# Hybrid attention / Mamba-2 kernel: tile 0's time steps inside layer 0's last output projection, and a first front that begins with context and tile 0

## The chip, the cores and the metric

The kernel runs on one core of one Trainium2 chip. The metric is device microseconds of one execution. A profile of one execution, taken by the hardware profiler, gives every instruction with its engine: PE (TensorE matmuls), DVE (VectorE), ACT (ScalarE), POOL (GpSimd) and SP (SyncE, whose queue issues most of the DMAs). Each engine takes its instructions in the order in which the program holds them.

## The reference

Two layers over a latent stream of 1024 tokens and a context of 256, model width 1024, all in float32. Layer 0 is gated windowed attention, layer 1 a bidirectional Mamba-2 (SSD) mixer. Each layer normalizes, modulates, mixes, and adds with a gate. What the change touches is the end of layer 0 and the beginning of layer 1:

```python
y, yc = attention_mixer(u, uc, ...)          # ends with (o * silu(g)) @ w_out
h = h + gate[:, None] * y
...
u = rms_normalize(h) * (1.0 + scale[:, None]) + shift[:, None]      # layer 1
...
z, xbc, dt_raw = jnp.split(h @ w_in, [SSD_WIDTH, SSD_WIDTH + SSD_CONV_DIM], axis=-1)
xbc = jax.nn.silu(centred_depthwise_conv(xbc, conv_w, conv_b))
xs, bm, cm = jnp.split(xbc, ...)
dt = jax.nn.softplus(dt_raw + dt_bias_dir)   # time steps: 2 directions x 32 heads
...
da = dt_d * a_dir[d]
a_cs = jnp.cumsum(da, axis=2)                # within chunks of 128 tokens
states = einsum(bm, exp(a_last - a_cs), xdt)
y_diag = (C B^T * exp(a_cs_q - a_cs_s)) @ xdt;  y_off = C @ h_prev * exp(a_cs)
```

The time steps `dt` of all tokens (64 rows: two directions by 32 heads) are needed by every one of the eight SSD groups; a group has four heads, 256 columns of x and of the gate z, and 128 each of B and C.

## The kernel before

**Tiling.** Tokens form three tiles, `TT`: latent tile 0 (512 tokens), latent tile 1 (512) and the context (256). The normalized, modulated stream of a layer is held as two parts in a reduced-precision format, `uH` and `uL`, one pair for each tile, with the model width on the partitions in eight slices; every projection multiplies high by high, high by low and low by high, so a product over width 1024 takes 24 matmuls for each output of 128 x 512.

**End of layer 0.** `attention` (lines of the functions below) works through blocks of queries; the output projections of the context and of tile 0 and the norm and modulation of layer 1 for them are woven between attention matmuls. Tile 1 comes last: `out_steps(1)` gives nine steps. Eight of them, `one(m)`, load two halves of a weight block of `wo`, split them (`wh` on ACT, `wl` on POOL, line 215), do 24 matmuls, add the gated result to the residual (`h1k`, DVE, line 696), store it, square it on ACT (line 703) and add the square to `sqa` on POOL (line 704). The ninth, `fin`, makes the norm from `sqa`: a matmul with ones (line 259), a square root on ACT (261), a reciprocal on DVE (262), and then for each of eight slices three operations (`modulate`, lines 294 to 296), which leave `uH` and `uL` of tile 1.

**Beginning of layer 1.** `ssd_consts` loads the small tables, then the time-step weight `w_dt`, and does the time-step projection of context, tile 0 and tile 1 (three times 24 matmuls with 64 output rows). The results go through a chain in two runs, first 768 columns (tile 0 and context), then 512 (tile 1): softplus on ACT and DVE with a change of ACT's function table between Ln and Exp, a scan over each chunk for each direction (lines 860, 861), two row tensors `acs` and `vrow` stored to DRAM, and three exponentials. Then for each chunk of 128 tokens two or three transposes on PE (lines 892, 895, 896) and copies by ACT (893, 897, 898) put the results into `dtdec`, `eacs` and `dtb`. PSUM holds these in three buffers, `psX`.

**Front of a group.** `front(g)` is a generator that yields after each matmul: four weight tiles in turn (B, two of x, C), each first on the context (in PSUM tile `psD`, one buffer; not for C), then on the latent tokens, tiles 0 and 1 alternating in one 1024-column PSUM tile (`pj2`, two buffers; the profile names it `pj`), then the gate z (line 1016). Each product goes through a depthwise convolution of five taps (`taps`: one on ACT, line 904, four on DVE, line 908), a silu (Tanh on ACT, line 915, a product on DVE, 916) and, but for C, transposes back into the same PSUM tile (line 955) with copies out of it by ACT (958). The PSUM tile is free for the next weight tile but one after the last copy. These steps are queued in `post` and popped as matmul time passes. Group 0's front runs alone; the fronts of the next groups are woven into the 64 slots of the scan.

**What sets the order.** The code is traced into a scheduler that places instructions on the engines by a simulated timeline; `high_priority(offset=...)` shifts a block's place and `issue_after(ins)` puts a block's instructions behind a given one on its engine.

Of the kernel before, what the change touches and what calls it, by code (L numbers as in the profile page):

```python
# [9 lines left out]
F32 = mybir.dt.float32  # L10
# [51 lines left out]
LATE = 3.0  # L62
SEGS = (1.5, 2.0, 2.0, 2.2, 2.2)
# [42 lines left out]
class Kernel:  # L106
# [116 lines left out]
    def mm3(self, ps, pairs, first=True, last=True):  # L223

        n = len(pairs)
        for i, (lh, ll, rh, rl) in enumerate(pairs):
            self.nc.tensor.matmul(ps, lh, rh, start=first and i == 0, stop=False)  # L227
            self.nc.tensor.matmul(ps, lh, rl, start=False, stop=False)  # L228
            self.nc.tensor.matmul(ps, ll, rh, start=False, stop=last and i == n - 1)  # L229
# [428 lines left out]
    def attention(self, c0, ckv):  # L658
# [21 lines left out]
        def out_steps(i):  # L680
# [4 lines left out]
            def one(m):  # L685
# [15 lines left out]
                else:  # L701
                    sq = t(p, [P, n], F32, "ut")
                    nc.scalar.activation(sq, h1, AF.Square)
                    nc.gpsimd.tensor_tensor(st["acc"], st["acc"], sq, op=ALU.add)
# [80 lines left out]
    def ssd_consts(self, p):  # L785
# [3 lines left out]
        dr = self.dr  # L789
# [17 lines left out]
        self.acs_d = t(dr, [2, 64, LAT], F32, "acs")  # L807
        self.v_d = t(dr, [2, 64, LAT], F32, "vrow")
# [3 lines left out]
        eal_d = t(dr, [1, 64, NT], F32, "eald")  # L812
        q = self.pdt
        wr = t(self.wp, [P, KT, P], F32, "wr")[:, :, :64]
# [15 lines left out]
        keep = keep.rearrange("p c n -> p (c n)")  # L830
        dts = t(q, [64, LAT + CTX], F32, "dt")
        where = {0: 0, 2: 512, 1: 768}
        for i in (2, 0, 1):
            n = TT[i][1]
            pj = self.proj(ps, (wh, wl), i, tag="psX", m=64)
            nc.scalar.activation(dts[:, where[i] : where[i] + n], pj[:64, :n], AF.Identity, bias=db)
        for lo, n, chunks in ((0, 768, (0, 1, 2, 3, 8, 9)), (768, 512, (4, 5, 6, 7))):
            nb = n // P
            dt = dts[:, lo : lo + n]
            if lo:  # L840
                q = self.pool("dtp2", ctx=self.cdt, side="right")
            w1, w2, w3 = [t(q, [64, n], F32, x) for x in ("w1", "w2", "w3")]

            nc.vector.scalar_tensor_tensor(w1, in0=dt, scalar=-1.0, in1=dt, op0=ALU.mult, op1=ALU.min)
            nc.scalar.activation(w1, w1, AF.Exp)
            nc.vector.tensor_scalar_add(w2, w1, 1.0)
            nc.vector.tensor_scalar_add(w3, w2, -1.0)
            nc.vector.tensor_sub(w1, w1, w3)
            nc.scalar.activation(w2, w2, AF.Ln)
            nc.scalar.activation(w3, w2, AF.Exp, scale=-1.0)  # L850
            nc.vector.tensor_mul(w1, w1, w3)
            nc.vector.tensor_add(w1, w1, w2)
            nc.vector.scalar_tensor_tensor(dt, in0=dt, scalar=0.0, in1=w1, op0=ALU.max, op1=ALU.add)
            ln = w2
            nc.vector.tensor_scalar_max(ln, dt, 1.0e-38)
            nc.scalar.activation(ln, ln, AF.Ln)
            da = w1
            nc.vector.tensor_scalar(out=da, in0=dt, scalar1=al, scalar2=None, op0=ALU.mult)
            acs = w3
            nc.vector.tensor_tensor_scan(out=acs[:32], data0=keep[:32, :n], data1=da[:32], initial=0.0, op0=ALU.mult, op1=ALU.add)  # L860
            nc.vector.tensor_tensor_scan(out=acs[32:, ::-1], data0=keep[32:, :n][:, ::-1], data1=da[32:, ::-1], initial=0.0, op0=ALU.mult, op1=ALU.add)
            def rows(dst, src):
                h = t(q, [64, 512], F32R, "rowh", 2)
                l = t(q, [64, 512], F32R, "rowl", 2)
                nc.scalar.copy(h, src[:, :512])
                nc.vector.tensor_sub(l, src[:, :512], h)
                for x, y in enumerate((h, l)):
                    nc.sync.dma_start(dst[x, :, chunks[0] * P : chunks[0] * P + 512], y.bitcast(F32))

            rows(self.acs_d, acs)  # L870
            av = acs.rearrange("p (c n) -> p c n", n=P)
            tot = t(q, [64, 6], F32, "tot")[:, :nb]
            nc.vector.tensor_copy(tot[:32], av[:32, :, P - 1])
            nc.vector.tensor_copy(tot[32:], av[32:, :, 0])
            et = t(q, [64, 6], F32, "et")[:, :nb]
            nc.scalar.activation(et, tot, AF.Exp)
            nc.sync.dma_start(eal_d[0][:, chunks[0] : chunks[0] + 4], et[:, :4])
            if nb > 4:
                nc.sync.dma_start(eal_d[0][:, 8:10], et[:, 4:])

            nc.vector.tensor_sub(ln, ln, acs)
            rows(self.v_d, ln)

            dd = w1
            nc.vector.tensor_sub(dd.rearrange("p (c n) -> p c n", n=P), tot.unsqueeze(2).broadcast_to([64, nb, P]), av)
            nc.scalar.activation(dd, dd, AF.Exp)
            nc.vector.tensor_mul(dd, dd, dt)
# [664 lines left out]
```

## Time and profile before

| | us |
|---|---|
| runs shown: median (lowest to highest of 3) | 1890.34 (1886.82 to 1890.7) |
| span of the profiled execution | 1886.0 |
| PE busy in it | 1790.8 (95%) |
| DVE, ACT, POOL busy | 1186.5, 906.5, 751.1 |
| attention ends, last projection's first blocks begin | about 722 |
| sixth of its eight blocks done | 765.0 |
| norm's matmul for tile 1 | 780.8 |
| first matmul of group 0's front | 791.8 |
| first gate (z) matmul of group 0 | 872.3 |

The profiled execution has no run time of its own in the list; its span stands beside the runs, the lowest of which lies 0.8 us above it. In the page, a busy share of PE does not say how far PE is from its peak, since matmuls are pipelined; what is read here is where PE sits idle, who ends the idle time, and how densely matmuls start after it. PE is busy in nearly every slice of 1/40 of the span, with lower digits at the beginning, in slices 17 and 18 (from 754 to 848) and at the end:

```profile
PE   6779998899999899879999999999999999999997
PEclk9889999999999999989999999999999999999998
```

### The profile page before, as it was taken

How to read it: one execution, taken by the hardware profiler on the slowest of the kernel's cores; microseconds unless marked ns; L12 is line 12 of the kernel's file. 1: busy time of each engine (PE TensorE's matmuls, PEld its weight loads, DVE VectorE, ACT ScalarE, POOL GpSimd, SP SyncE). 2: the span in 40 equal slices, each digit the busy share in tenths (PEclk: the TensorE clock that was granted, in tenths of full speed). 3: DMA queues.
4: the chain of work that ended last, by engine and by line, in shares of the span. 5: the costliest groups of instructions: out<-in, count | busy, mean ns of one | idle time of the engine just before them, and what ended most of it. 6: DMA issues, size and time to landing. Idle time of an engine off the chain costs nothing. (4 is left out here: it accounts for less than half of the span.)

```text
span 1886.0 us, 29647 instructions
## 1 busy us (share of the span) xinstructions
PE 1790.8 (95%) x10632; PEld 1543.2 (82%) x10632; DVE 1186.5 (63%) x2214; ACT 906.5 (48%) x1863; POOL 751.1 (40%) x1026
## 2 busy tenths in 40 slices
PE   6779998899999899879999999999999999999997
PEld 3678776788889787668898898989889898988887
DVE  4753425887777766584665757666575766754743
ACT  4522225677787765472353534434353543543532
POOL 2731105664456464302334352524335252442411
PEclk9889999999999999989999999999999999999998
DMA  9338765653345456220111111111111111433552
GB/s 358 111 79 251 233 209 132 143 124 95 96 118 135 112 137 198 87 55 23 49 36 44 44 36 44 36 44 36 43 47 33 44 39 41 138 119 100 176 162 68
DMA packets 147204, 192.10 MB, mean 102 GB/s; under 512 B 15313, under 2 KB 84817, under 8 KB 147057
## 3 DMA queue, kind: packets, MB, share of 16 engines
q1 hardware_dynamic: 112992, 171.56, 29.1%
q0 software_dynamic: 34064, 18.65, 5.6%
q8 instruction: 84, 1.38, 0.3%
q14 instruction: 64, 0.52, 0.1%
HBM read 154.54 MB, written 35.92 MB: 101 GB/s over the span
## 5 line engine op out<-in xcount | busy, mean ns | idle before, releaser
L227 PE MATMUL pj<-uH,wh 128*128 128x512 f32 (+1 forms) x712 | 258.8, 365 | 27.1 <-DVE v L549 9.5
L228 PE MATMUL pj<-uL,wh 128*128 128x512 f32 (+1 forms) x712 | 245.6, 345 | 1.5 <-DVE uL L441 1.2
L229 PE MATMUL pj<-uH,wl 128*128 128x512 f32 (+1 forms) x712 | 245.0, 344 | 1.3 <-POOL wl L215 1.3
L1066 POOL TENSOR_TENSOR xw<-xn,dtdec 128x256 f32<-128x256 f32 x144 | 106.4, 741 | 205.7 <-PE psD L1089 102.5
L227 PEld LDWEIGHTS pj<-uH,wh 128*128 128x128 f32 x712 | 136.9, 193 | 55.8 <-issue 19.1
L991 PE MATMUL pj<-uH,wh 128*128 128x512 f32 x512 | 171.7, 405 | 0.8 <-ACT xn L958 0.8
L991 PE MATMUL pj<-uH,wl 128*128 128x512 f32 x512 | 171.7, 404 | 0.0
L991 PE MATMUL pj<-uL,wh 128*128 128x512 f32 x512 | 168.7, 399 | 0.0
L215 POOL TENSOR_TENSOR wl<-wr,wh 128x512 fp32r<-128x512 f32 x96 | 125.7, 1313 | 97.9 <-ACT wh L213 97.2
L1016 PE MATMUL pj<-wh,uH 128*128 128x256 f32 x512 | 154.7, 302 | 0.0
L638 DVE TENSOR_TENSOR pl<-pt,ph 128x512 fp32r<-128x512 f32 x168 | 114.4, 688 | 63.5 <-ACT ph L637 62.8
L1016 PE MATMUL pj<-wh,uL 128*128 128x256 f32 x512 | 151.4, 296 | 0.0
L1016 PE MATMUL pj<-wl,uH 128*128 128x256 f32 x512 | 151.0, 295 | 0.0
L229 PEld LDWEIGHTS pj<-uH,wl 128*128 128x128 f32 x712 | 136.3, 192 | 17.7 <-POOL wl L215 1.7
L228 PEld LDWEIGHTS pj<-uL,wh 128*128 128x128 f32 x712 | 137.1, 193 | 15.7 <-DVE uL L441 3.6
L213 ACT CAST wh<-wr 128x512 fp32r<-128x512 f32 (+1 forms) x136 | 86.9, 644 | 124.7 <-PE pj L228 88.0
L1195 ACT ACTIVATE uT<-psX,nw 128x128 f32<-128x128 f32 x128 | 47.0, 367 | 189.8 <-PE psX L1194 188.6
L612 DVE CUSTOM_DVE_ANT_0 sm<-S,mask,nsink 128x640 f32<-128x640 f32 (+2 forms) x160 | 119.2, 772 | 23.2 <-PE S L609 11.9
L637 ACT CAST ph<-pt 128x512 fp32r<-128x512 f32 x168 | 97.3, 585 | 61.3 <-PE pt L633 55.6
L614 ACT ACTIVATE sm<-sm,nm 128x640 f32<-128x640 f32 (+2 forms) x160 | 118.6, 742 | 11.0 <-DVE nm L612 10.4
L1161 POOL TENSOR_TENSOR xs<-xn,sk 128x256 f32<-128x256 f32 x64 | 42.0, 656 | 184.7 <-DVE sk L1157 183.4
L991 PEld LDWEIGHTS pj<-uL,wh 128*128 128x128 f32 x512 | 95.6, 188 | 19.9
(332 smaller groups left out, 4994.8 us busy)
## 6 DMA issues: line engine op xcount, KB each, us to landing
wr<-w_x SPq DMA_DIRECT2D x32, 512.0 KB
wr<-wo SPq DMA_DIRECT2D x48, 256.0 KB
wr<-w_sk SPq DMA_DIRECT2D x24, 512.0 KB
wr<-wg SPq DMA_DIRECT2D x40, 256.0 KB
qs<-q POOLq DMA_DIRECT2D x40, 256.0 KB, 3.9
wada<-w_ada SPq DMA_DIRECT2D x16, 512.0 KB
wr<-wq SPq DMA_DIRECT2D x32, 256.0 KB
wl<-w_ada SPq DMA_DIRECT2D x32, 256.0 KB
```

Source lines behind the costliest of these rows:

```text
L213: nc.scalar.copy(h, raw)
L215: (eng or nc.vector).tensor_tensor(l, raw, h, op=ALU.subtract)
L227: self.nc.tensor.matmul(ps, lh, rh, start=first and i == 0, stop=False)
L228: self.nc.tensor.matmul(ps, lh, rl, start=False, stop=False)
L229: self.nc.tensor.matmul(ps, ll, rh, start=False, stop=last and i == n - 1)
L612: nc.vector.tensor_tensor_reduce(out=sm[:, :W], in0=Sv, in1=self.mask[:, m0 : m0 + W], scale=-SCALE, scalar=self.nsink[:, 4 * j + r : 4 * ...
L614: nc.scalar.activation(sm[:, :W], sm[:, :W], AF.Exp, bias=nm[:, r : r + 1], scale=-1.0, accum_out=sums[:, r : r + 1])
L637: nc.scalar.copy(ph, ptf)
L638: nc.vector.tensor_sub(pl, ptf, ph)
L991: nc.tensor.matmul(raw[:, 512 * i : 512 * i + 512], l[:, k, :], r[i][:, k, :], start=k + y == 0, stop=k == KT - 1 and y == 2)
L1016: nc.tensor.matmul(pj[:, c], l, r[:, k, :], start=c % 2 + q + k + y == 0, stop=c % 2 == 1 and q == 1 and k == 3 and y == 2)
L1066: nc.gpsimd.tensor_tensor(xw, X(st, c).rearrange("p (r h) -> p r h", r=R), self.dtdec[:, c, hd(d, g)].unsqueeze(2).broadcast_to([P, R, HP] ...
```

## The change

It has five parts.

1. **Time steps inside the projection.** The loads and the split of `w_dt` and the constants move out of `ssd_consts` into `dt_setup`, called ahead of the last projection; the time-step weight now uses that projection's weight pool. After the sixth of the eight blocks, tile 0's time-step matmuls follow (`dt_proj(0)`), and the chain is traced for its 512 columns. After the eighth block the context's matmuls follow (`dt_proj(2)`), and the norm's matmul is put behind them.
2. **The last addition to `sqa`** goes to DVE in place of POOL.
3. **The chain in two runs of another cut:** 512 columns (tile 0), then 768 (tile 1 and context), which stay in `ssd_consts`, with `dt_proj(1)` ahead of them. The transposes become a function `spread`, called with priority for tile 0, and for the rest when the front of group 0 has yielded `DTLATE` = 40 us of matmul time by its own count.
4. **Front of group 0.** It begins with the context and tile 0 of the B tile, tile 0 of the first x tile, and then does tile 1 of the B tile, the context and tile 1 of the x tile. The other groups keep their order.
5. **Pools.** The gate's buffers get a pool of their own; the scan's pool, its constants and the first `load_rows` come after the late `spread`; one row buffer for each of high and low in place of two.

```diff
+DTLATE = 40.0
...
-                    nc.gpsimd.tensor_tensor(st["acc"], st["acc"], sq, op=ALU.add)
+                    (nc.vector if i == 1 and m == KT - 1 else nc.gpsimd).tensor_tensor(st["acc"], st["acc"], sq, op=ALU.add)
...
-            for f in out_steps(1):
+            steps = out_steps(1)
+            self.dt_setup()
+            for m, f in enumerate(steps[:-1]):
                 for _ in f():
+                    pass
+                if m == 5:
+                    with self.tc.issue_after(self.mm.ins):
+                        self.dt_proj(0, "pt")
+                    self.dt_first = self.dt_chain(0, 512, (0, 1, 2, 3))
+            with self.tc.issue_after(self.mm.ins):
+                mm = self.dt_proj(2, "pt")
+            with self.tc.issue_after(mm.ins):
+                for _ in steps[-1]():
                     pass
...
+        with self.tc.high_priority(offset=-150):
+            self.dt_proj(1, "psX")
+        with self.tc.high_priority(offset=-200):
+            self.dt_first()
+        last = self.dt_chain(512, 768, (4, 5, 6, 7, 8, 9))
+        return last
...
+    def dt_proj(self, i, tag):
+        s, n = TT[i]
+        pj = self.proj(self.psA, self.wdt, i, tag=tag, m=64)
+        mm = self.mm
+        self.nc.scalar.activation(self.dts[:, s : s + n], pj[:64, :n], AF.Identity, bias=self.db)
+        return mm
...
-                h = t(q, [64, 512], F32R, "rowh", 2)
-                l = t(q, [64, 512], F32R, "rowl", 2)
+            h = t(q, [64, 512], F32R, "rowh", 1)
+            l = t(q, [64, 512], F32R, "rowl", 1)
...
+        if g == 0:
+            need(w)
+            w0, w = w, loads[1]()
...
+            yield from context(0, w0)
+            r0 = tokens(tiles[0][1])
+            yield from mm(r0[0], w0, both[:1])
+            need(w)
+            w1, w = w, loads[2]()
...
+            r1 = tokens(tiles[1][1])
+            yield from mm(r1[0], w1, both[:1])
+            yield from mm(r0[0], w0, both[1:])
+            finish(0, *r0)
+            yield from context(1, w1)
+            yield from mm(r1[0], w1, both[1:])
+            finish(1, *r1)
+            n = 2
...
-            sz = t(p, [P, 4, 256], F32, "sz")
+            sz = t(self.pz, [P, 4, 256], F32, "sz")
...
+        work = self.front(0, st, post)
+        while done < DTLATE:
+            cost = next(work)
+            post.run(cost)
+            done += cost
+        spread()
+        self.cdt.close()
+        self.pz = self.pool("sz", ctx=c0)
+        ps2 = self.pool("scan", ctx=c0)
```

How the scheduler places this shows at two places. The first is ACT's queue at the norm of tile 1: `ut` is the Square of a block of the projection (the last named one belongs to the eighth block), `sqa` the square root, `w` and `rowh` belong to the time-step chain, and `dt` is the bias of a time-step projection. Before:

```order
L213 CAST wh_8631<-wr_8629 128x512
L213 CAST wh_8637<-wr_8635 128x512
L703 ACTIVATE ut_8626<-h1k_8597 128x512
L703 ACTIVATE ut_8670<-h1k_8641 128x512
L261 ACT_TABLE_LOAD
L261 ACTIVATE sqa_8675<-pj_8673,eps_70 128x512
```

The changed kernel:

```order
L885 ACT_TABLE_LOAD
L885 ACTIVATE w_2140_8632<-w_2140_8632 64x512
L894 CAST rowh_8649<-w_2141_8633 64x512
L905 ACT_TABLE_LOAD
L905 ACTIVATE et_8658<-tot_8655 64x4
L915 ACTIVATE w_2139_8631<-w_2139_8631 64x512
L917 ACTIVATE w_2141_8633<-w_2141_8633 64x512
L894 CAST rowh_8662<-w_2140_8632 64x512
L704 ACTIVATE ut_8757<-h1k_8728 128x512
L859 ACTIVATE dt_8341<-pt_8760,db_8331 64x256
L262 ACT_TABLE_LOAD
L262 ACTIVATE sqa_8788<-pj_8786,eps_70 128x512
```

The second half of tile 0's chain, with its table loads, now stands ahead of the last Square and so of the square root.

The second place is PE where the transposes of tile 0's time steps stand (`psX` is their PSUM buffer, `pj` the 1024-column tile of a weight tile of the front, `bT` the B tile). Before:

```order
L991 MATMUL pj_2232_9150<-uH_2148_8678,wl_9090 128x512
L892 MATMUL psX_8885<-ident_63,w_2181_8843 128x64
L892 MATMUL psX_8892<-ident_63,w_2181_8843 128x64
L892 MATMUL psX_8899<-ident_63,w_2181_8843 128x64
L895 MATMUL psX_8885<-ident_63,w_2183_8845 128x64
L896 MATMUL psX_8885<-ident_63,dt_8764 128x64
L895 MATMUL psX_8892<-ident_63,w_2183_8845 128x64
```

The changed kernel:

```order
L1012 MATMUL pj_2220_9042<-uH_2169_8791,wl_8986 128x512
L990 MATMUL pj_2217_9004<-ident_63,bT_9005 128x128 x4
L927 MATMUL psX_8891<-ident_63,w_2141_8633 128x64
L928 MATMUL psX_8891<-ident_63,dt_8341 128x64
L927 MATMUL psX_8898<-ident_63,w_2141_8633 128x64
L928 MATMUL psX_8898<-ident_63,dt_8341 128x64
L927 MATMUL psX_8905<-ident_63,w_2141_8633 128x64
L928 MATMUL psX_8905<-ident_63,dt_8341 128x64
L990 MATMUL pj_2217_9004<-ident_63,bT_9005 128x128 x4
L1012 MATMUL pj_2229_9208<-uH_2061_8258,wh_9155 128x512
```

All transposes of the time steps stood in one run behind the first x tile; now tile 0's are spread among the front's matmuls, and the B tile's transposes come ahead of the second x tile, which takes over their PSUM tile.

More of the change, by code (lines that the diff above doesn't have):

```diff
@@ L228, in mm3 @@
             self.nc.tensor.matmul(ps, lh, rl, start=False, stop=False)
[L229 removed]
+            self.mm = self.nc.tensor.matmul(ps, ll, rh, start=False, stop=last and i == n - 1)
     def proj(self, pspool, w, i, tag="pj", m=P):
@@ L829, in ssd_consts @@
         nc.vector.memset(keep[32:, :, P - 1 : P], 0.0)
[L830 to L862, printed above, removed]
-                h = t(q, [64, 512], F32R, "rowh", 2)
-                l = t(q, [64, 512], F32R, "rowl", 2)
[L865 to L887, printed above, removed]
-            nc.scalar.activation(acs, acs, AF.Exp)
@@ new lines, in mm @@
+        def mm(raw, w, parts):
+            for k in range(KT):
+                for y, (l, r) in enumerate(((w["h"], uH), (w["h"], uL), (w["l"], uH))):
+                    for i, o, n in parts:
+                        nc.tensor.matmul(raw[:, o : o + n], l[:, k, :], r[i][:, k, :], start=k + y == 0, stop=k == KT - 1 and y == 2)
+                        yield N512 if n == 512 else N256
+                if k == 3 and parts[-1][0] == 1 and w is not hold[0]:
+                    post.extend(hold[1]["steps"])
```

150 lines of the change are left out of this document (108 added, 42 removed).

## The prediction

> **What bounds the kernel now.** I read the busy time by stretches first, then the TensorE timeline of the stretch that the change touches, then ACT and DVE in the same stretch. The columns of the first view are: stretch, its length, busy us and count of PE, PE's weight loads, DVE, ACT and POOL, granted TensorE clock, DMA share, GB/s.
>
> ```profile
> 765.03:872.27 107.24, 91.46 (x449) 73.05 (x448) 73.11 (x97) 58.23 (x102) 12.95 (x12) 0.92 0.15 43
> ...
> 900.00:1800.00 900.00, 895.60 (x5445) 798.91 (x5444) 585.12 (x1061) 398.04 (x799) 355.38 (x517) 1.00 0.20 61
> ...
> 830.00:840.00 10.00, 9.63 (x55) 8.64 (x55) 9.75 (x11) 7.28 (x29) 0.00 (x0) 0.58 0.25 60
> ```
>
> From 900 on PE idles 4.4 us in 900: whatever is won or lost before that reaches the end whole, because the same matmuls follow. Between 765.03 (sixth of eight blocks of the last output projection done) and 872.27 (first gate matmul of group 0) it idles 107.24 - 91.46 = 15.8 us, and part of its busy time is at half rate. That stretch is what the change rebuilds. Its PE rows give start, length and, in brackets, the idle time ahead and who ended it:
>
> ```profile
> 765.03 0.39 PE L227 MATMUL pj<-uH,wh 128*128 128x512 f32 x1
> ...
> 766.97 0.51 PE L229 MATMUL pj<-uH,wl 128*128 128x512 f32 x1 [1.31 <-POOL wl L215]
> ...
> 780.78 2.08 PE L259 MATMUL pj<-sqa,ones 128*128 128x512 f32 x2 [2.99 <-POOL sqa L704]
> ...
> 784.07 0.28 PE L229 MATMUL psX<-uH,wdtl 128*64 128x256 f32 x1
> ...
> 785.97 0.40 PE L227 MATMUL psX<-uH,wdth 128*64 128x512 f32 x1
> ...
> 791.51 0.40 PE L227 MATMUL psX<-uH,wdth 128*64 128x512 f32 x1
> ...
> 822.56 0.40 PE L892 MATMUL psX<-ident,w 64*128 64x64 f32 x3 [0.46 <-DVE w L887]
> 829.85 0.36 PE L895 MATMUL psX<-ident,w 64*128 64x64 f32 x1 [6.89 <-ACT dtdec L893]
> ...
> 834.29 0.58 PE L982 MATMUL psD<-uH,wh 128*128 128x256 f32 x1
> ...
> 838.43 0.28 PE L982 MATMUL psD<-uL,wh 128*128 128x256 f32 x1
> ...
> 841.15 0.66 PE L955 MATMUL pj<-ident,cacc 128*128 128x128 f32 x4 [1.05 <-ACT xn L958]
> ...
> 870.94 0.66 PE L955 MATMUL pj<-ident,cacc 128*128 128x128 f32 x4 [1.60 <-ACT xn L958]
> ...
> 872.27 0.56 PE L1016 MATMUL pj<-wh,uH 128*128 128x256 f32 x1
> ```
>
> Two waits carry it: 2.99 us for the sum of squares under layer 1's norm, and 0.46 + 6.89 us at the transposes of the time steps. After both, matmuls come at half rate (the granted clock of 830 to 840 is 0.58). A 512-column matmul takes (791.51 - 785.97) / 24 = 0.23 us, a 256-column one about 0.12. From 780.78 to 784.07 PE started two norm matmuls and eight of 256 columns: about 0.46 + 8 x 0.12 = 1.4 us of work in 3.3, so 1.9 lost. From 834.29 to 838.43 it did 19 of 256 columns, 2.3 us of work in 4.1: 1.9 lost; the 25 small transposes of 829.85 to 834.29 took 4.4 against some 2.8 at 0.11 each, less 0.3 of idle already counted: 1.4 lost. In all the stretch holds 15.8 + 1.9 + 1.9 + 1.4 = 21.0 us that are not work.
>
> **Part 1: the time-step work moved into the projection.** No matmul is added or dropped. The 24 time-step matmuls of tile 0 (5.5 us) now follow the sixth block, so the 1.31 us wait of the next block's weights is covered: its POOL subtraction was done 2 us after 765.03. The 24 of the context (24 x 0.12 = 2.9 us) follow the eighth block and lie over the 2.99 us wait. Were nothing else moved, both waits would be gone. But the first 512 columns' softplus, scan and exponentials are moved too, and by the order they stand ahead of the last block's Square on ACT and of its residual on DVE. Their pieces:
>
> ```profile
> 804.27 0.68 DVE L844 SCALAR_TENSOR_TENSOR w<-dt 64x512 f32<-64x512 f32 x1 [0.18 <-ACT dt L836]
> ...
> 805.88 0.41 DVE L846 TENSOR_SCALAR w<-w 64x512 f32<-64x512 f32 x1
> ...
> 820.57 0.47 DVE L858 TENSOR_SCALAR w<-dt,al 64x512 f32<-64x512 f32 x1
> ...
> 777.83 0.75 DVE L696 SCALAR_TENSOR_TENSOR h1k<-S,mod,h1k 128x512 f32<-128x512 f32 x1 [4.74 <-PE S L229]
> ...
> 823.67 1.22 DVE L861 TENSOR_TENSOR_SCAN w<-keep,w 32x512 f32<-32x512 f32 x1
> ...
> 815.16 0.62 ACT L865 CAST rowh<-w 64x512 fp32r<-64x512 f32 x1 [2.03 <-DVE w L861]
> ...
> 818.04 0.21 ACT L876 ACTIVATE et<-tot 64x6 f32<-64x6 f32 x1
> ...
> 822.10 0.63 ACT L856 ACTIVATE w<-w 64x512 f32<-64x512 f32 x1
> ...
> 778.69 0.63 ACT L703 ACTIVATE ut<-h1k 128x512 f32<-128x512 f32 x1 [4.88 <-DVE h1k L696]
> 779.34 1.28 ACT L261 ACT_TABLE_LOAD   x1
> ...
> 779.46 1.26 POOL L704 TENSOR_TENSOR sqa<-sqa,ut 128x512 f32<-128x512 f32 x1 [3.78 <-ACT ut L703]
> ```
>
> Tile 0's matmuls end at 765.03 + 5.5 + 0.2 = 770.7. Then in turn: ACT bias 0.7, DVE 0.7, ACT Exp 0.6 (772.7); ACT cast of a weight 0.6, load 1.28, Ln 0.63, load 1.28, Exp 0.63 (777.1); DVE three of 0.68, the seventh block's residual (0.75), 0.41 and 0.47, the last two partly overlapping (780.6); the two scans, 2.4 (783.0); ACT cast 0.6, load 1.28, a small Exp 0.2, two Exp and a cast at 0.6 (786.9); then the last Square 0.63 and the last addition, which the change gives to DVE (0.7 in place of POOL's 1.26): 788.3. PE is there at 765.03 + 3 x 5.5 + 2.9 = 784.4. **New wait at the norm: 3.9 us, where 2.99 stood,** and half rate after it (1.9) as before. Behind the waiting matmul PE holds the context and tile 0 of the front, which need nothing of the norm but come in order; what waits for it in turn is the square root on ACT and DVE's reciprocal. Bounds: 0, if the seventh block's residual and the copies cost nothing extra; above, the 768-column chain of before, which shared DVE with others (below), 8 us more.
>
> The Trainium skill, "ScalarE: Activation LUTs", section "What ACT_TABLE_LOAD costs", gives a load 1.28 us and a drain of 1.38 behind it, 2.66 in all. The load agrees with the row; a drain does not show here, for the norm's load, like the others, is followed by an instruction that waits for data only. With the page's figure the four loads would put this wait at 3.9 + 4 x 1.38 = 9.4 us.
>
> **Part 2: the front begins with context and tile 0.** The second tile's time steps were filler before while u of tile 1 was made:
>
> ```profile
> 782.89 0.69 ACT L261 ACTIVATE sqa<-pj,eps 128x512 f32<-128x512 f32 x1 [2.27 <-PE pj L259]
> 783.61 3.35 DVE L262 RECIPROCAL sqa<-sqa 128x512 f32<-128x512 f32 x1 [5.03 <-ACT sqa L261]
> 787.00 5.39 DVE L294 SCALAR_TENSOR_TENSOR h1k<-h1k,mod,sqa 128x512 f32<-128x512 f32 x8
> 792.30 5.39 DVE L296 SCALAR_TENSOR_TENSOR uL<-h1k,mod,uH 128x512 fp32r<-128x512 f32 x8
> ```
>
> The first uL slice is there 12.2 us after the norm's matmul starts, the last at 16.9. The new filler is context (2.9) and tile 0 for two weight tiles (5.5 each): 13.9 us, plus the norm matmul and the 1.9 of half rate. PE needs u of tile 1 some 16 us after the norm and finds six slices; one slice feeds three matmuls (0.69) and takes DVE 0.67. No wait here. Cost 0; it would be up to 2 us if the one convolution tap that the order puts between the slices came late.
>
> **Part 3: the waits behind it.** The transposes of tile 0's time steps are now scattered among matmuls with their inputs ready since 786.9: the 0.46 + 6.89 + 0.30 go, with 3.3 of half rate. In their place the second chain (768 columns: tile 1 and context) shares DVE and ACT with the convolutions, and the two 1024-column PSUM tiles (`pj2`) must be emptied in time. Rows:
>
> ```profile
> 828.52 1.19 ACT L904 ACTIVATE cacc<-pj,cb,cw 128x1024 f32<-128x1024 f32 x1
> ...
> 862.47 1.03 ACT L915 ACTIVATE pj<-cacc 128x1024 f32<-128x1024 f32 x1 [3.27 <-DVE cacc L908]
> ...
> 819.20 0.85 ACT L886 ACTIVATE w<-w 64x768 f32<-64x768 f32 x1 [0.44 <-DVE w L885]
> ...
> 829.61 0.41 ACT L893 COPY dtdec<-psX 128x64 f32<-128x64 f32 x3
> ...
> 839.11 1.05 ACT L931 CAST wh<-wr 128x1024 fp32r<-128x1024 f32 x1 [1.29 <-PE psD L982]
> ...
> 840.52 0.57 ACT L958 COPY xn<-pj 128x512 f32<-128x512 f32 x1
> ...
> 797.61 0.94 DVE L844 SCALAR_TENSOR_TENSOR w<-dt 64x768 f32<-64x768 f32 x1
> ...
> 813.38 1.75 DVE L861 TENSOR_TENSOR_SCAN w<-keep,w 32x768 f32<-32x768 f32 x1
> ...
> 829.74 5.24 DVE L908 SCALAR_TENSOR_TENSOR cacc<-pj,cw,cacc 128x1022 f32<-128x1022 f32 x4 [0.86 <-ACT cacc L904]
> ```
>
> First handover (the B tile's). PE goes from 804.4 through second halves, tile 1's time steps and the second context and wants the transposes at 825.2. DVE has the four taps (5.2) and the product done by 821.5, so they run; but ACT, from about 821.7, first has load 1.28, Ln 0.85, three small copies 0.4, load 1.28, Exp 0.85, a weight's cast 1.05 and the next tile's L904 1.19: the copy-out of the first half ends at 829.1, the second at 830.3. PE, with 0.4 + 0.7 of transposes to do, waits 2.8 + 0.8 us, and goes on at half rate, as it did behind 2.99 us: 1.9. Second handover (first x tile): two scans of 1.75 and six operations near 0.94 lie between its taps; the product is ready at 845.7, when PE is too, and three short waits for ACT follow (0.5, 0.8, 1.2). Third: ACT's next L904 comes ahead of a copy, 1.4 + 0.6. Before, the longest waits of this kind were 1.05 and 1.60. Each of the three is bounded below by 0 and above by 6.89, the wait behind a whole chain; I keep the walk, which is nearest to those rows.
>
> The other edits cost nothing in PE time: one row buffer in place of two only delays a 64x512 cast that nobody on PE waits for; the gate tile's own pool and the later opening of the scan pool move loads that land 20 us ahead of use. The five stores of the first chain pass SP ahead of the gate weights, which are needed 80 us later. POOL only loses the last addition. Of the moved loads, 0.25 MB of time-step weight now pass SP ahead of the first block's weights instead of ahead of the fourth's; the cover is that a block lasts 5.5 us. I allow 1 us either way.
>
> **Sum.** Gone: 21.0. New: 3.9 + 1.9 + 2.8 + 0.8 + 1.9 + 2.5 + 2.0 = 15.8. Gain 5.2 us. The profiled span goes from 1886.0 to 1880.8; the median of the runs shown, 1890.34, lies 4.3 above that span, and I carry the difference: **1885.1 us**.
>
> **Rivals.** *The handovers become the bound.* Speaking for it: DVE is busy 9.75 of 10 us and more than before stands between taps. If each of the three costs the 6.89 of the old wait, they sum to 20.7 in place of 8.1: 12.6 more, 1897.7 us, slower. It decides from 13.3 us for the three. Against it: 10 us of the chains now run while DVE is otherwise idle. *The norm waits for the whole chain.* In the old trace the 768-column chain took from 797.61 to 820.05, 22.4 us, against the 14.4 I count from its first to its last Exp: 8 more, 1893.1 us, no change. Against it: at 770 nothing else is on DVE. By the skill's drain, with 5.5 more, it would be 1890.6, also no change. *More is hidden.* If the three handovers cost 1.60 each, there is no half rate behind the first, and the norm waits 2 us: 3.3 + 1.9 + 1.9 = 7.1 less, 1878.0. *It does not do what it says:* the scheduler could have left tile 0's matmuls behind the norm; the order of PE excludes it.
>
> **Numbers.** 0.2% (3.8 us) is about what a measurement of this kernel tells from no change. The forecast (1882 to 1888) has 0.50, of which 0.45 lies below 1886.5; more hidden 0.15; the norm's wait 0.20; the handovers 0.15. So faster 0.60, same 0.25, slower 0.15. The range 1877 to 1894 leaves out half of the slow case and a part of the fast one.
>
> **What would show it.** Right: a PE idle of 3 to 5 us ahead of the norm's matmul, ended by DVE in place of POOL; no wait over 1 us between that and the B tile's transposes; waits of 2 to 4 us there, ended by ACT copies; the first gate matmul near 866 on the old time axis; PE idle of 11 to 13 us in the rebuilt stretch. Wrong: a norm wait over 8 us; one of the handovers at 6 us or more; new idle time after 900; or the first block of the projection starting late behind the moved weight.

## The result, and the profile after

| | median of runs, us | lowest to highest | ratio to before (95%) |
|---|---|---|---|
| before | 1890.52 (4 runs) | 1886.82 to 1891.68 | |
| changed | 1918.07 (4 runs) | 1916.38 to 1920.56 | 1.0139 (1.0124 to 1.0155) |

The change makes the kernel 27.6 us slower; 5.2 us faster was forecast. Two views by stages show where. The stages are: up to one matmul of the attention (its 61st `pv`), up to its last `pv`, up to the end of the sixth projection block, up to the first gate matmul of group 0, up to the last gate matmul, the rest. The columns are those of the first view of the prediction. Before:

```profile
0.00:470.10 470.10, 419.61 (x2397) 336.14 (x2398) 269.22 (x557) 214.35 (x471) 197.85 (x249) 0.96 0.60 174
470.10:729.30 259.20, 251.73 (x1519) 216.05 (x1518) 187.05 (x404) 189.88 (x418) 143.49 (x204) 0.99 0.45 118
...
872.27:1659.00 786.73, 783.32 (x4975) 709.81 (x4974) 511.22 (x933) 338.91 (x685) 316.81 (x476) 1.00 0.16 48
1659.00:1886.00 227.00, 211.13 (x1166) 182.68 (x1164) 118.77 (x193) 85.68 (x159) 64.43 (x75) 0.97 0.39 123
```

The changed kernel:

```profile
0.00:476.60 476.60, 425.15 (x2397) 340.30 (x2398) 269.57 (x557) 214.00 (x471) 198.13 (x249) 0.95 0.59 172
476.60:737.10 260.50, 252.11 (x1518) 216.06 (x1517) 186.19 (x404) 190.07 (x418) 143.57 (x204) 0.99 0.44 117
...
773.13:881.05 107.92, 94.31 (x452) 72.99 (x450) 76.84 (x97) 58.23 (x101) 16.23 (x14) 0.92 0.15 43
881.05:1688.60 807.55, 789.52 (x4956) 712.14 (x4955) 516.22 (x928) 330.79 (x681) 309.41 (x468) 0.99 0.16 46
1688.60:1918.50 229.90, 212.74 (x1185) 183.68 (x1183) 124.24 (x199) 86.94 (x164) 68.17 (x80) 0.98 0.39 122
```

The two profiled spans differ by 32.5 us. Of these 6.5 lie in the first stage, where both kernels hold the same instructions in the same order; among the runs below this stage ends anywhere from 468.5 to 478.4, so it is no part of the change. The rebuilt stretch takes 107.92 in place of 107.24: it won nothing. The loss is **behind** it: 807.55 - 786.73 = 20.8 us in the stages of the groups (with 19 matmuls fewer recorded by their end), and 2.9 in the tail. From the end of the attention on, where the two stretches can be compared, the profiles take 1918.5 - 737.1 = 1181.4 and 1886.0 - 729.3 = 1156.7 us: 24.7 more.

The rebuilt stretch on PE (start, length, idle time ahead and its releaser):

```profile
800.60 2.08 PE L260 MATMUL pj<-sqa,ones 128*128 128x512 f32 x2 [7.94 <-DVE sqa L705]
...
842.91 1.11 PE L990 MATMUL pj<-ident,bT 128*128 128x128 f32 x4 [2.20 <-ACT bn L993]
...
862.84 0.66 PE L990 MATMUL pj<-ident,cacc 128*128 128x128 f32 x4 [0.73 <-ACT xn L993]
864.04 0.27 PE L927 MATMUL psX<-ident,w 64*128 64x64 f32 x1 [0.55 <-ACT dtdec L925]
...
879.49 0.66 PE L990 MATMUL pj<-ident,cacc 128*128 128x128 f32 x4 [1.39 <-ACT xn L993]
```

The norm waits 7.94 us, not 3.9. Why it does stands on DVE (with the POOL and ACT rows beside it):

```profile
778.33 4.54 POOL L705 TENSOR_TENSOR sqa<-sqa,ut 128x512 f32<-128x512 f32 x3
781.74 1.40 DVE L876 TENSOR_SCALAR w<-w 64x512 f32<-64x512 f32 x1
783.18 1.68 DVE L877 TENSOR_TENSOR w<-w,w 64x512 f32<-64x512 f32 x1
...
789.11 1.60 POOL L705 TENSOR_TENSOR sqa<-sqa,ut 128x512 f32<-128x512 f32 x1 [4.80 <-ACT ut L704]
789.59 1.40 DVE L884 TENSOR_SCALAR w<-dt 64x512 f32<-64x512 f32 x1
...
797.56 0.62 ACT L704 ACTIVATE ut<-h1k 128x512 f32<-128x512 f32 x1
799.26 0.68 DVE L895 TENSOR_TENSOR rowl<-w,rowh 64x512 fp32r<-64x512 f32 x1 [1.82 <-DMA acs<-rowl]
799.87 0.68 DVE L705 TENSOR_TENSOR sqa<-sqa,ut 128x512 f32<-128x512 f32 x1
```

Two things are seen. Three operations of the chain that took 0.41, 0.68 and 0.41 us in the kernel before (its L847, L848 and L855) take 1.40, 1.68 and 1.40, with POOL at work. And the last Square is done at 798.2, but the addition starts at 799.87: it stands behind the second row subtraction, which waits until the first row's store has left the only buffer.

Now the groups. The largest waits are at the start of the gate (z). PE, DVE and ACT there, in group 4:

```profile
1307.27 1.04 ACT L966 CAST wh<-wr 128x1024 fp32r<-128x1024 f32 x1
1307.40 0.89 DVE L1184 COPY_PREDICATED psX<-before,psX 128x256 f32<-128x256 int32 x2 [2.31 <-PE psX L1183]
...
1308.47 1.22 ACT L939 ACTIVATE cT<-pj,cb,cw 128x1024 f32<-128x1024 f32 x1
...
1309.97 0.81 ACT L1175 CAST rrow<-rraw 32x768 fp32r<-32x768 f32 x1
1310.69 0.37 ACT L1185 ACTIVATE M<-psX 128x256 f32<-128x256 f32 x1
...
1311.11 0.80 PE L1195 MATMUL psX<-cT,bT 128*128 128x128 f32 x2 [2.74 <-ACT M L1185]
1311.58 0.58 PE L1088 MATMUL pj<-wh,uH 128*128 128x256 f32 x1
```

The stretch behind that wait and one whole group from gate to gate, by windows:

```profile
1311.11:1314.00 2.89, 2.89 (x13) 2.89 (x14) 2.89 (x5) 0.94 (x3) 0.00 (x0) 0.50 0.56 206
...
1425.88:1539.04 113.16, 110.28 (x683) 98.97 (x682) 72.79 (x132) 46.32 (x98) 43.00 (x66) 0.98 0.14 39
```

The slot's first matmul (L1195) waits for the Exp (L1185). The Exp's data are there at 1308.3, when the weight's cast ends, but on ACT it stands behind four more operations: the first tap of C (L939), the cast of the rows (L1175) and two short ones (0.37 and 0.51 us). So PE idles 2.74 us and then runs at half the clock (0.50). In the kernel before the Exp of the same slot (L1127) ran ahead of that cast:

```profile
1292.44 0.37 ACT L1127 ACTIVATE M<-psX 128x256 f32<-128x256 f32 x1
...
1294.25 0.38 PE L1137 MATMUL psX<-cT,bT 128*128 128x128 f32 x2
...
1294.46 1.05 ACT L931 CAST wh<-wr 128x1024 fp32r<-128x1024 f32 x1
```

A group takes 113.16 us from gate to gate, with 2.9 of them idle. Before it took less, and with 0.5 idle:

```profile
1407.20:1515.70 108.50, 108.02 (x684) 97.56 (x683) 71.06 (x132) 47.59 (x97) 43.62 (x67) 1.00 0.14 41
```

So of the 4.7 us more, 2.4 are idle time and 2.3 matmuls at the lower clock.

### The profile page after: what moved, and what is told of

The parts are those of the page before. It is cut to its first block, busy times and chain, and to the rows that moved or that the text cites. A ratio compares the mean times of both kernels' runs of the same rounds, so it can differ in the third digit from the quotient of the medians.

```text
span 1918.5 us, 29651 instructions
## 1 busy us (share of the span) xinstructions
PE 1806.3 (94%) x10632; PEld 1549.3 (81%) x10632; DVE 1199.3 (63%) x2215; ACT 898.9 (47%) x1863; POOL 750.1 (39%) x1025
## 5 line engine op out<-in xcount | busy, mean ns | idle before, releaser
L1124 POOL TENSOR_TENSOR xw<-xn,dtdec 128x256 f32<-128x256 f32 x144 | 98.1, 684 | 274.6 <-PE psD L1147 129.6
L228 PEld LDWEIGHTS pj<-uH,wh 128*128 128x128 f32 x712 | 137.2, 193 | 55.5 <-issue 19.1
L230 PEld LDWEIGHTS pj<-uH,wl 128*128 128x128 f32 x712 | 136.3, 192 | 17.1 <-POOL wl L216 1.1
L615 ACT ACTIVATE sm<-sm,nm 128x640 f32<-128x640 f32 (+2 forms) x160 | 118.6, 742 | 11.9 <-DVE nm L613 11.6
L1012 PEld LDWEIGHTS pj<-uH,wh 128*128 128x128 f32 x512 | 94.7, 190 | 21.1 <-ACT bn L993 3.0
```

The lines of the kernel that those rows point to most:

```text
L230: self.mm = self.nc.tensor.matmul(ps, ll, rh, start=False, stop=last and i == n - 1)
L615: nc.scalar.activation(sm[:, :W], sm[:, :W], AF.Exp, bias=nm[:, r : r + 1], scale=-1.0, accum_out=sums[:, r : r + 1])
L1012: nc.tensor.matmul(raw[:, o : o + n], l[:, k, :], r[i][:, k, :], start=k + y == 0, stop=k == KT - 1 and y == 2)
L1124: nc.gpsimd.tensor_tensor(xw, X(st, c).rearrange("p (r h) -> p r h", r=R), self.dtdec[:, c, hd(d, g)].unsqueeze(2).broadcast_to([P, R, HP] ...
```

## The experiments

From the first slot on the change edits nothing but the pool of the gate's buffers and the function of the front, which gives the other groups the steps that it gave before; both kernels trace the same instructions there. But the scheduler places them by its simulated timeline, and puts the slots elsewhere between the front's matmuls. Counted in the order: how many matmuls behind the group's first gate matmul the first matmul of each of the group's own eight slots stands, for group 4.

```
before, e1, e5, e7, e10          256 369 440 509 591 652 725 793
e4 (front's cost 3% larger)      257 371 440 515 591 652 725 793
e11, e12 (decays' priority)      261 370 440 509 591 652 725 795
changed                          287 399 468 542 607 681 752 827
e2 (nothing of the change), e6, e8 279 398 490 561 624 715 783 855
e3                               309 401 486 540 611 689 766 831
```

Three theories: **order** (this placing costs the 24 us behind the first gate matmul), **memory** (the new pools make the slots wait), **moved work** (norm's wait and handovers).

**e1: the changed kernel, slots put back by a delay.**

```diff
         M = t(ps2, [P, R, P], F32, "M")
+        for _ in range(32):
+            nc.vector.memset(M, 0.0)
         round_rows(0)
```

> The changed kernel with 32 memsets of 128x512 on DVE ahead of the first slot's decays. In program order nothing else moves; but the first slots then stand later, and from the second slot on every slot's matmuls stand where the kernel before had them. Order theory (the later groups are slower because the slots' matmuls stand some 20 matmuls later between the front's than before, and wait at the start of the gate behind ACT's work there): the waits of 2.3 to 2.7 us for ACT's Exp ahead of the first gate matmul go, a group takes 108.5 us as before, and what is left is the first front, some 2.5 us late, and what the memsets cost: 1893 us (1889 to 1900). Memory theory (the gate's own pool and the later scan pool make the slots wait): 1916 to 1922, the waits stay. Theory of the moved work (norm's wait and handovers are what costs): 1916 to 1922, since none of it is touched.

Measured: 1891.95 us (10 runs), ratio 1.0009 (0.9993 to 1.0025). Its rebuilt stretch and one group:

```profile
767.20:874.70 107.50, 93.83 (x451) 72.47 (x450) 78.90 (x102) 58.23 (x101) 16.30 (x14) 0.94 0.15 42
...
1407.50:1516.00 108.50, 108.02 (x683) 97.57 (x682) 71.07 (x132) 47.59 (x97) 43.62 (x67) 1.00 0.14 41
```

All pools and all moved work are still there, and the 26 us are gone. Memory and moved work fall as causes of the loss; the change itself, with the old placing, is worth nothing measurable.

**e2: the kernel before, 40 memsets at the same place.**

> The kernel before with 40 memsets of 128x512 on DVE ahead of the first slot's decays, no part of the change in it. The delay throws the slots of all later groups into other places between the front's matmuls, up to some 80 matmuls from where they stood. Order theory: waits of 2 us and more appear around the start of the gate in most groups, 1905 to 1920 us. Memory theory and theory of the moved work: 1890 us plus what the memsets hold up at one place, at most 8 us: 1890 to 1898.

Measured: 1915.25 us, 1.0128 (1.0107 to 1.0150).

```profile
875.30:1671.30 796.00, 783.10 (x4931) 704.66 (x4930) 516.07 (x929) 333.45 (x674) 298.33 (x460) 1.00 0.16 46
1671.30:1912.30 241.00, 221.58 (x1211) 190.03 (x1209) 127.82 (x212) 90.75 (x172) 75.29 (x92) 0.96 0.39 119
```

Without any part of the change the same size of loss, in another shape: 9.3 us up to the last gate matmul, with 44 matmuls fewer done by then, and 14.0 in the tail.

**e3: the kernel before, the chain cut the other way.**

```diff
-        where = {0: 0, 2: 512, 1: 768}
+        where = {1: 0, 0: 512, 2: 1024}
...
-        for lo, n, chunks in ((0, 768, (0, 1, 2, 3, 8, 9)), (768, 512, (4, 5, 6, 7))):
+        for lo, n, chunks in ((0, 512, (4, 5, 6, 7)), (512, 768, (0, 1, 2, 3, 8, 9))):
...
+        self.pz = self.pool("sz", ctx=c0)
...
-            sz = t(p, [P, 4, 256], F32, "sz")
+            sz = t(self.pz, [P, 4, 256], F32, "sz")
```

Besides, the row buffers are one each, as in the change.

> The kernel before, with only the chain of the time steps cut the other way (512 columns of tile 1 first, then 768), one row buffer in place of two, and the gate's buffers in a pool of their own. No projection is moved and the first front is the old one; but the slots of the later groups stand elsewhere. Order theory: 1903 to 1920 us, with the waits in the later groups and none new before 870 us. Memory theory: by the gate's pool alone 1890 to 1895, since the scan's pool opens where it did. Theory of the moved work: 1888 to 1893.

Measured: 1913.31 us, 1.0119 (1.0096 to 1.0142). Order holds, though some 6 us of this are its own: the first gate matmul comes 149.1 us behind the last attention matmul, in the kernel before 143.0. PE waits longer at the time steps' transposes than the 0.46 + 6.89 us of before, so the expectation of nothing new ahead of 870 failed.

```profile
838.71 0.58 PE L892 MATMUL psX<-ident,w 64*128 64x64 f32 x3 [12.53 <-DVE w L887]
```

**e4: the changed kernel, slots spread over a front taken 3% larger.**

```diff
-                    work, total = self.front(g + 1, nst, post, st.get("next")), FRONT
+                    work, total = self.front(g + 1, nst, post, st.get("next")), FRONT * 1.03
```

> The changed kernel, with the front's cost per group that the slots are spread over taken 3% larger. The first two groups stand as in the changed kernel, from the third on the slots stand within 6 matmuls of where the kernel before had them. Order theory: the waits go from the third group on, 1895 to 1902 us. Memory theory and theory of the moved work: 1914 to 1922 us.

Measured: 1895.93 us, 1.0019 (1.0003 to 1.0034), as order expects; from the third group's gate on a group takes 108.6 to 108.9 us.

**e5 and e6: two buffers for the low rows of tile 0's chain, 4 memsets or 3.**

```diff
-            l = t(q, [64, 512], F32R, "rowl", 1)
+            l = t(q, [64, 512], F32R, "rowl", 1 if lo else 2)
...
+        for _ in range(4):
+            nc.vector.memset(M, 0.0)
```

In e6 the 4 is a 3.

> The changed kernel with two buffers again for the low rows of tile 0's chain alone, and 4 memsets of 128x512 on DVE ahead of the first slot, which put the slots of all later groups where the kernel before had them. Norm's wait: in the changed kernel the last addition to sqa stands on DVE behind the second row subtraction, which idles 1.82 us until the first row's store has left the one buffer. Row-buffer theory: this idle time goes, norm's matmul waits 6.1 to 6.4 us in place of 7.9. Rival (the chain's length alone makes the addition late): 7.9 stays. Time: order theory 1888 to 1893; memory theory 1914 or more.

> The kernel before this one in the list with 3 memsets in place of 4: a memset of 128x512 less on DVE, everything else the same, but the slots of the later groups stand 15 to 80 matmuls from where they stood. Order theory: 20 to 28 us slower than with 4, 1908 to 1918. Any theory that prices what is computed, moved or stored: the same time as with 4 memsets, within 1 us.

Measured: e5 1888.08 us, 0.9983 (0.9967 to 0.9998); e6 1915.76 us, 1.0117 (1.0089 to 1.0146). The norm of e5, and the stages behind the first gate matmul of e6:

```profile
795.32 2.07 PE L260 MATMUL pj<-sqa,ones 128*128 128x512 f32 x2 [6.26 <-DVE sqa L705]
```

```profile
881.60:1675.60 794.00, 782.90 (x4933) 705.07 (x4934) 511.20 (x916) 335.06 (x676) 300.31 (x459) 1.00 0.16 47
1675.60:1916.70 241.10, 221.54 (x1211) 190.05 (x1209) 127.80 (x212) 90.62 (x172) 75.24 (x91) 0.96 0.38 118
```

The row buffer's part of the norm's wait is 1.7 us (7.94 - 6.26). And one memset of DVE more or less is worth 27.7 us: e6 has the places of e2 in the table, and a tail like that of e2 with the groups within 2 us, though one holds the change and the other does not.

**e7: the chain cut behind the softplus.** The scans and the rest are traced behind the eighth block and tied behind its Square and addition; two row buffers; 32 memsets.

```diff
+            with self.tc.issue_after(self.sqi.ins), self.tc.issue_after(self.adi.ins):
+                self.dt_first = half()
             with self.tc.issue_after(self.mm.ins):
                 mm = self.dt_proj(2, "pt")
```

> The changed kernel with tile 0's chain cut in two behind the softplus: the scans and what follows are put behind the last Square on ACT and the last addition on DVE; two buffers for the low rows of this chain; 32 memsets ahead of the first slot, which put the later groups' slots where the kernel before had them. Chain theory (what stands ahead of the last Square and addition makes norm wait, and the half rate behind it): the addition comes as soon as the eighth block's residual is there, norm waits 0 to 0.7 us in place of 7.9 and the half rate behind it goes; up to 3 us come back, since the rest of the chain stands between the reciprocal and u of tile 1. First gate matmul 137 to 140 us behind the last attention matmul in place of 144; 1883 to 1888 us. Rival (the rest of the chain only moves and delays u of tile 1 by as much): 1889 to 1893.

Measured: 1884.03 us, 0.9955 (0.9940 to 0.9970): faster than both kernels, 7.8 us by the medians of its own series (the kernel before 1891.78).

```profile
788.95 1.12 PE L260 MATMUL pj<-sqa,ones 128*128 128x512 f32 x2 [0.56 <-DVE sqa L705]
...
832.16 1.11 PE L995 MATMUL pj<-ident,bT 128*128 128x128 f32 x4 [3.93 <-ACT bn L998]
```

```profile
766.40:869.50 103.10, 93.73 (x463) 72.87 (x462) 80.69 (x104) 58.53 (x103) 18.26 (x15) 0.97 0.17 47
```

Of the norm's wait 0.56 is left, the first handover's has grown from 2.20 to 3.93, and the stretch is 4.1 us shorter than before the change. The first gate matmul comes 137.0 us behind the last attention matmul (143.0 before the change), as the chain theory has it.

**e8: the changed kernel with the old front.**

```diff
-        if g == 0:
+        if g == -1:
```

> The changed kernel with group 0's front in the old order (context, then tiles 0 and 1 of a weight tile alternating). Only the stretch up to the first gate matmul is read, since the later groups stand elsewhere again. Cover theory (the new front gives PE 11 us of work while u of tile 1 is made): PE waits 8 to 11 us more behind the norm, and the first gate matmul comes 150 to 156 us behind the last attention matmul in place of 144. Rival (the new order of the front saves nothing): 143 to 146.

Measured in one run: from the norm's matmul to the first gate matmul 85.9 us (793.85 to 879.7) against 80.4 in the changed kernel; from the last attention matmul 149.3. With the old front:

```profile
793.85:879.71 85.86, 77.96 (x355) 60.99 (x355) 58.31 (x74) 41.83 (x79) 3.22 (x5) 0.87 0.12 32
```

The rival falls, but the cover theory holds no better: with the old front PE waits 0.97 us for u of tile 1, not 8 to 11. In the changed kernel PE is busy 74.78 us from 800.60 to 881.05, with the same 355 matmuls and a clock of 0.93. So of the 5.5 us that the old front is longer, 2.2 are idle time and 3.2 the same matmuls at a lower clock, and this is one run. (1910.05 us in all, from group 4 on with the places of e2.)

**e9: DVE beside POOL.**

> A measurement by itself, nothing of the reference is computed: twelve operations of each of three kinds on DVE (an addition of a constant, a subtraction of two tensors, a scalar-tensor-tensor operation, all 64x512 in float32), first alone, then beside a row of sixteen 128x512 additions on POOL. In the changed kernel two rows of the chain's constant additions took 1.40 us where the same operation took 0.41 in the kernel before, with POOL at work only in the first. Port theory (DVE and POOL hold the way to the memory against each other): the constant addition takes 0.41 us alone and 1.0 to 1.4 beside POOL; the other two kinds 0.68 alone and 0.7 to 1.4 beside it. Rival (the long rows come from the operations' own dependence on each other): the same time alone and beside POOL.

Measured, by groups of lines (times it ran, busy us, mean ns; L93 and L97 alone, L105 and L109 beside POOL; the third kind took what the subtraction took):

```profile
L121 POOL TENSOR_TENSOR g<-g,h 128x512 f32<-128x512 f32 x48 | 70.6, 1471 | 3.8
L109 DVE TENSOR_TENSOR u<-u,v 64x512 f32<-64x512 f32 x12 | 19.6, 1632 | 0.4
...
L105 DVE TENSOR_SCALAR u<-u 64x512 f32<-64x512 f32 x12 | 16.4, 1366 | 0.4
L97 DVE TENSOR_TENSOR u<-u,v 64x512 f32<-64x512 f32 x12 | 8.2, 682 | 0.4
...
L93 DVE TENSOR_SCALAR u<-u 64x512 f32<-64x512 f32 x12 | 5.0, 419 | 0.4
```

Each kind takes 0.95 us more beside POOL, as the long rows of the chain did; the two-input kinds more than I had allowed.

**e10: e7 with the second chain at 100 places less priority, 4 memsets.**

> The kernel with the chain of tile 0 cut in two (as in the faster kernel of the run before), and besides the second chain (768 columns) traced with 100 places less priority; 4 memsets ahead of the first slot in place of 32 put the later groups' slots where the kernel before had them. The copy-out of the B tile's first half stands on ACT ahead of the second table load of that chain, no longer behind it and its Exp. Theory (the first handover waits for what stands ahead of the copy on ACT): the wait of 3.93 us at the B tile's transposes falls to 1.5 to 2.5, the first gate matmul comes 134 to 136 us behind the last attention matmul in place of 137, 1880 to 1886 us. Rival (the table load and Exp come back as a wait at the next handover): 137 to 138 us, 1883 to 1888 us.

Measured: 1884.45 us, 0.9954 (0.9936 to 0.9973), the time of e7. The waits at that handover are 2.46 and 1.86 in place of 0.95, 3.93 and 0.68, and the first gate matmul comes 134.9 us behind the last attention matmul in place of 137.0, as the theory has it; but the next gate comes 99.7 us later in place of 98.6, and the tail takes 228.9 in place of 226.9. The 1.1 us go with the memsets and not with this edit (98.6 in e1 and e7 with 32, 99.7 in e5 with 4); e5, with the same places from group 1 on, has a tail of 228.2. So the edit helps where it was made, and the totals do not tell the two kernels apart.

**e11 and e12: the decays first.** In e11 the changed kernel, in e12 e10 without memsets:

```diff
+            with self.tc.high_priority(offset=30):
                 for d in range(2):
                     nc.tensor.matmul(o[:, d], rrow[:, 4 + d], rrow[:, 2 * half : 2 * half + 2], start=True, stop=True)
                 nc.vector.copy_predicated(o[:, 0], self.before.unsqueeze(1).broadcast_to([P, 2, P]), o[:, 1])
                 nc.scalar.activation(M[:, 2 * half : 2 * half + 2], o[:, 0], AF.Exp)
```

> The changed kernel with nothing added: only the decays of a slot (two matmuls, the predicated copy and the Exp) are traced with 30 places more priority. By the order the first two groups stay as in the changed kernel, from the third on the slots stand within 5 matmuls of where the kernel before had them, and in the last group, beside the output projection, 10 to 38 matmuls later. Order theory: the waits of 2.3 to 2.7 us for the Exp go, groups three to seven take 108.5 us; 1893 to 1903 us, the last group's places being the open part. Any theory that prices the moved work, the pools or the memory: 1914 to 1922 us.

> The kernel with tile 0's chain cut in two and the second chain at less priority, without memsets, and with the decays traced with 30 places more priority. By the order the later groups' slots stand within 7 matmuls of those of the kernel before from the second group's second slot on, but the last group's 10 to 38 later. Order theory: first gate matmul 134 to 136 us behind the last attention matmul, 108.5 us for a group, 1881 to 1888 us if the last group's places cost little, up to 1897 if they cost what the last group of the kernels with 40 and with 3 memsets lost behind the last gate matmul (some 13 us against the kernel before).

Measured: e11 1894.54 us, 1.0012 (0.9997 to 1.0026); e12 1885.74 us, 0.9958 (0.9940 to 0.9976), its first gate matmul 136.3 us behind the last attention matmul, a little outside the expectation.

```profile
872.30:1659.70 787.40, 781.48 (x4962) 707.53 (x4961) 512.75 (x934) 338.66 (x684) 315.33 (x471) 1.00 0.16 48
```

This is e11 between its gates: 787.4 us, where the changed kernel took 807.55. No delay is added here, so it is not the memsets that heal. From the last attention matmul to the end e11 takes 1163.2 us (1156.7 before, 1181.4 in the changed kernel): 18 of the 24.7 us come back. Most of the other 6.5 stand in the tail, 232.4 against 227.0, where the last group's places are not the old ones.

## Why the prediction was wrong

**The step that failed** is in its first part: "whatever is won or lost before that reaches the end whole, because the same matmuls follow". The same matmuls follow, but not in the same places. Some 24 of the 27.6 us are this: 20.8 between the gates and 2.9 in the tail, and e1 takes them away with the change untouched. No rival had it; "new idle time after 900" stood only among what would prove the forecast wrong. The cost of a group (113.2 in place of 108.5, for the group that was shown) is one Exp behind other operations on ACT, with the clock's price on top: e11 gives the Exp and what feeds it priority, and from the third group on a group takes 108.5 again.

**The rebuilt stretch** was forecast 5.2 us shorter and is 0.7 longer.

- Norm's wait: 3.9 forecast, 7.94 measured. The mechanism (the chain ahead of the last Square and addition) was right, as e7 shows: without it 0.56. The size was wrong in two places. The step "one row buffer in place of two only delays a 64x512 cast that nobody on PE waits for" failed: 1.7 us (e5), since the addition stands behind that row on DVE. The other 2.4 are the walk itself, which took DVE's durations from rows with POOL idle; three operations beside POOL took 1 us more each. By the rows 1.9 of these 3 us lie on the way to the addition (ACT's table load at 784.94 waits 0.94 us for the 1.68 us row, and the 1.40 us row of L884 delays the scans by 1.0), and 0.5 is the weight's cast of 781.43, which waits 0.49 us for PE. e9 shows the price beside POOL, but the split is read from rows and not shown by a run: the additions on POOL were not taken away in the kernel.
- The rival "the norm waits for the whole chain" (11.9 us) was as far off on this wait, on the other side, and its reason, sharing DVE with other work of DVE, is not what is seen. The rival of a drain behind each table load (9.4 us) is out: the load at 794.61 takes 1.28 us, and the Exp behind it starts at 795.90.
- Part 2, no wait while u of tile 1 is made: right, no row over 0.3 us between 800.6 and 842.9. How much the new order of the front is worth stays open: e8 took 5.5 us more without it, but hardly by a wait for u.
- The handovers: 2.8 + 0.8, 2.5 and 2.0 forecast, 2.20 + 0.68, 0.73 + 0.55 and 1.39 measured, ended by ACT's copies as forecast; 2.5 us too high together. The rival of slow handovers (20.7 us) is out.
- The clock: 3.8 us of half rate forecast. PE is busy 94.31 us for some 86.2 of work (107.24 less the 21.0 of the forecast), so 8.1 are lost: about 2.4 behind the norm (11.4 us at 0.79), about 3 behind the first handover (4.42 busy us at half rate in a row whose 0.57 counts the wait too, then 14 us at 0.94), and by estimate 1.8 at six transposes of time steps that stand singly between matmuls of 512 columns. From 834.91 to 835.78 two such matmuls and a transpose take 0.87 us, where twice 0.23 and the 0.11 of a transpose among transposes make 0.57; the forecast put nothing down for scattering them. Some 0.9 are not split up. (Of the 25 small transposes that the forecast counts from 829.85 to 834.29 in the kernel before, there are 23; this moves its 21.0 by 0.2.) Nor is the half rate behind a wait a fixed price: it did not follow the same 2.20 us wait in e11 (last row below), nor the norm's 2.99 us in e2 (1.00 from 783.64 to 787).

```profile
800.60:812.00 11.40, 11.40 (x50) 9.45 (x51) 8.53 (x9) 5.64 (x9) 0.00 (x0) 0.79 0.05 12
...
842.00:848.00 6.00, 4.42 (x12) 3.37 (x13) 6.00 (x9) 4.42 (x12) 0.00 (x0) 0.57 0.29 87
848.00:862.00 14.00, 14.00 (x75) 11.81 (x73) 12.03 (x14) 6.72 (x10) 0.00 (x0) 0.94 0.27 62
```

```profile
834.36:838.00 3.64, 2.96 (x14) 2.33 (x15) 3.64 (x6) 2.73 (x9) 0.00 (x0) 1.00 0.47 131
```

With both faults of the norm's wait out and the old placing (e7) the stretch is 4.1 us shorter, of the 5.2 forecast: the forecast's mechanism was there, but not in the kernel as it was changed. The kernel is 7.8 us faster; of the rest, 2.1 stand between the first two gates (98.6 us in place of 100.7, as in e1, so by the places of group 0's slots), and 1.9 between the attention and the sixth block, whose cause is open.

## What to carry to other kernels

Where a scheduler places instructions by a simulated timeline, an edit at one end can move instructions that it does not touch: compare the order of the untouched part first, and if it moved, price that before the edit. A steady pattern can be lost by a single memset, so judge an edit with the pattern held (a small delay, or a priority on the operation that others wait for), and only then ask what the edit is worth. When walking a chain through an engine, take durations from rows with the same neighbours at work, and ask of each saved buffer what stands behind its wait.

## What the runs showed of the hardware

- A DVE operation of 64x512 in float32 takes 0.42 (one input) or 0.68 us (two) alone, and 1.37 or 1.63 beside POOL's additions, which themselves go from about 1.26 each to 1.41 (22.6 / 16) or 1.61 (25.8 / 16), means of rows of sixteen whose last four ran alone. The Trainium skill, "SBUF — State Buffer", section "Who interferes with whom", has a rule for it: such operations and POOL's reads take the shared port pair as a lock, and the other blocks. The measurement agrees that each holds up the other; the forecast had left the rule out.
- PE runs at half its clock behind waits of 2.20 us (842.91) and of 2.74 (1311.11), but not behind 1.39 (879.49, in a stretch at 1.00). The length of the wait does not decide it alone: behind 2.20 us in e11 and 2.99 in e2 the clock was 1.00. The Trainium skill, "TensorE: Matmul & The Clock Gate", section "What's actually happening", gives about 3.4 us of idle window for this; here shorter waits were enough, though not each time.
- The first stage, the same instructions in the same order, takes 468.5 to 478.4 us from run to run: two profiles are to be compared from a common point on.
